# A packed copy of the queries, and a later start, in the recurrent mixer of a two-layer encoder

## The chip, the cores and the metric

One Trainium2 chip; the kernel runs on one of its cores. The metric is the device time of one execution in microseconds (us). Engines are named as the profile names them: PE is TensorE (matmuls; PEld its weight loads), DVE is VectorE, ACT is ScalarE, POOL is GpSimd, SP is SyncE, whose queue issues the loads of weights.

## The reference, cut to what matters

Two sequences, of 512 and 256 tokens (768 together), run through the same trunk of two layers with a model width of 1024, all in fp32. A layer adds half a SwiGLU feed-forward block, a token mixer and again half a feed-forward block to the residual x. The mixer of layer 0 is a bidirectional gated linear recurrence (HGRN2) with 8 heads of 128; that of layer 1 is windowed attention. Of the recurrence, in one direction and for one head:

```python
q, i, g, f_fw, f_bw = jnp.split(x @ w_in, 5, axis=-1)
f = lbd + (1.0 - lbd) * jax.nn.sigmoid(fpre)      # the gate of one direction
k = 1.0 - f
# S_t = diag(f_t) S_{t-1} + k_t v_t^T,  o_t = S_t^T q_t
o = o_fwd + rev(o_bwd)                            # the same, run from the other end
```

So o_t is a sum over all tokens s: the product of q_t and k_s, weighted by the product of the gates between s and t, times v_s.

## The kernel before, in words

All of the work is one program, unrolled by Python, for 768 tokens in 6 blocks of 128. It is a chain of stages: feed-forward f0, the mixer `hgrn`, f1, f2, windowed attention `swa`, f3. The instructions are written in program order with Python generators that weave pieces of different work; a scheduler then fixes the order on each engine at compile time. It may take a later written instruction first if that one is ready in its model and the earlier one isn't. Waits between engines are set by it as well.

Products of the feed-forward blocks and projections split each fp32 operand in a high and a low part and make three matmuls (`mm3`, lines 260 to 262, high times high, high times low, low times high). Weights come in by DMA (line 151), ACT casts the high part (line 166) and DVE subtracts (line 167); `done` frees a weight and stages the next.

The mixer works head by head. `hgrn_proj` makes for one head the projections for the queries (weights with c0 = 0) and the two gates (c0 = 3 and 4), each for the 512 tokens and then for the 256 tokens. It is a generator: it yields after each two of the eight inner tiles for the 512 tokens (4 pieces, the last one behind the evacuation, line 673) and twice for the 256 tokens (2 pieces). So a head's projection has 3 x 6 = 18 pieces. At its end it makes the gates f, the keys k = 1 - f (line 680) and the products q = qs * f of the queries and the gates (line 681), for two directions, which lie one behind the other in one tile of 2 x 768 columns per partition.

`hgrn_scan` computes the outputs of one head in seven levels. At level l the tokens are taken in groups of J = 2^l: the two halves of each pair of groups see each other through gates multiplied up to there. For that, at each level:

- ACT copies the keys that are wanted, alternating between the two directions in runs of J columns, to `kop` (line 717, in the same tile as the matrix A);
- PE makes the scores of the six blocks of 128 tokens: stationary `kop`, moving `rhs(b)`, which reads the queries directly from q with the same alternating pattern, runs of J columns (line 692, in `scan_scores`). Each of these fp32 matmuls stands as two records in the trace;
- DVE puts the scores into A (line 706 copies at level 0, line 711 copies under a mask);
- at level 0 alone PE also makes the diagonal scores from `kd` and `qs`, which lie in order (line 692 too, put by line 711);
- DVE multiplies q (line 734), k (line 738) and the running products of gates `totals` (line 740) for the next level.

After the levels the keys are transposed (line 754, evacuated by line 755), the states of the blocks are made (line 762, then lines 770 and 773), and the outputs are summed from A, q and the states (line 786). ACT squares them (line 790) and copies them over the values (line 792), DVE reduces the squares (line 793).

`hgrn` weaves: the projection of head 0 is made first, then 4 pieces of the projection of head 1 (`lead`), and then each scan is run with 18 pieces of the feed spread evenly over its eight steps (`weave`); the scan of head 3 has 24 more, as the second half of the values' projection is there. The last scan has the projection of the output gates (`proj_tok("g0", ...)`) beside it.

Tiles named "big" share 21 slots of 6 KB per partition; a tile takes a slot when it is first written and gives it back after its last use. Among them are the 8 tiles of h (the mixer's input), the masks, qk, f, q and k of each head, ka (with kop and A), totals, kT and S.

Of the kernel before, what the change touches and what calls it, by code (L numbers as in the profile page):

```python
# [16 lines left out]
P = 128  # L17
# [5 lines left out]
T = TA + TB  # L23
NBLK = T // P
EPS = 1e-6
HEADS = 8
# [13 lines left out]
RAWBUFS = 4  # L40
SLOTS = 21
RING = 1024
UP = ("p1", "p7", "p2", "p5", "p4", "p6", "p3")
DOWN = ("p1", "p2", "p5", "p4", "p7", "p6", "p3")
FACTOR = {"p1": "b00", "p2": "b10", "p3": "b11", "p4": "t4", "p5": "t1", "p6": "t2", "p7": "t3"}
# [2 lines left out]
class Trunk:  # L48
# [344 lines left out]
    def plan_ffn(self, tag, w1, w2):  # L393
        def up(i):
# [4 lines left out]
            else:  # L399
                self.plan_quad((tag, i), (gate, up), (NC, P), UP)  # L400

# [292 lines left out]
    def hgrn_scan(self, hd, v):  # L694
        nc = self.nc
        h, qs, kd, f, q, k = (hd[n] for n in ("h", "qs", "kd", "f", "q", "k"))
        ka = self.big([P, 2, T])
        kop, A = ka[:, 0, :], ka[:, 1, :]
        totals = self.big([P, 2, T])
        blk = lambda t, b: t[:, b * P : (b + 1) * P]  # L700

        def put(level, pss):
            for s, (off, n) in enumerate(SEQS):
                dst = A[:, off : off + n]
                if level == 0:
                    nc.vector.tensor_copy(dst, pss[s])
                    continue
                nb = n // P
                m = self.masks[:, level, :].unsqueeze(1).to_broadcast([P, nb, P])
                r = lambda t: t.rearrange("p (b j) -> p b j", b=nb)  # L710
                nc.vector.copy_predicated(r(dst), m, r(pss[s]))

        tot, base = f, 0
        for l in range(LEVELS):
            c, J = T >> l, 1 << l
            kv = bass.AP(k.tensor, k.offset, [list(k.ap[0]), [2 * J, c // 2], [T + J, 2], [1, J]])
            nc.scalar.copy(kop.rearrange("p (b g j) -> p b g j", g=2, j=J), kv)

            def rhs(b):
                return bass.AP(  # L720
                    q.tensor, q.offset + b * P, [list(q.ap[0]), [2 * J, P // (2 * J)], [T + J, 2], [1, J]]
                )

            pss = [self.ps(n) for _, n in SEQS]
            self.scan_scores(pss, lambda b: blk(kop, b), rhs)
            put(l, pss)
            if l == 0:
                pss = [self.ps(n) for _, n in SEQS]
                self.scan_scores(pss, lambda b: blk(kd, b), lambda b: blk(qs, b))
                put(LEVELS, pss)  # L730
            part = [list(q.ap[0])]
            both = bass.AP(q.tensor, q.offset, part + [[T + J, 2], [2 * J, c // 2], [1, J]])
            t = bass.AP(tot.tensor, tot.offset + base + 1, [list(tot.ap[0]), [T - 1, 2], [2, c // 2], [0, J]])
            nc.vector.tensor_mul(both, both, t)
            for d in range(2):
                xv = self.halves(k, l, d, d)
                t = tot[:, 1 - d, base + 1 - d : base + c : 2].unsqueeze(2).to_broadcast([P, c // 2, J])
                nc.vector.tensor_mul(xv, xv, t)
            nbase = 0 if l == 0 else base + c
            nc.vector.tensor_mul(  # L740
                totals[:, :, nbase : nbase + c // 2], tot[:, :, base : base + c : 2], tot[:, :, base + 1 : base + c : 2]
            )
            tot, base = totals, nbase
            yield

        F, Bk = 1, 0
        order = ((0, 0), (0, 1), (0, 2), (0, 4), (1, 1), (1, 2), (1, 3), (1, 5))
        kT = self.big([P, 8, P])
        S = self.big([P, 8, P])
        for half in range(2):  # L750
            pt = self.ps()
            for i in range(4):
                d, b = order[half * 4 + i]
                nc.tensor.transpose(pt[:, i * P : (i + 1) * P], blk(k[:, d, :], b), self.ident)
            nc.scalar.copy(kT[:, half * 4 : half * 4 + 4, :], pt.rearrange("p (a b) -> p a b", a=4))
        vb = lambda b: v[b][:, h * P : (h + 1) * P]
        pds = []
        for half in range(2):
            pd = self.ps()
            for i in range(4):  # L760
                d, b = order[half * 4 + i]
                nc.tensor.matmul(pd[:, i * P : (i + 1) * P], kT[:, half * 4 + i, :], vb(b), start=True, stop=True)  # L762
            pds.append(pd)
        state = {}
        for d, steps in ((0, ((0, None), (1, 0), (2, 1), (4, None))), (1, ((3, None), (2, 3), (1, 2), (5, None)))):
            for b, prev in steps:
                i = order.index((d, b))
                ds = pds[d][:, (i % 4) * P : (i % 4 + 1) * P]
                if prev is None:
                    nc.scalar.copy(S[:, i, :], ds)  # L770
                else:
                    dec = totals[:, 1 - d, base + b : base + b + 1]
                    nc.vector.scalar_tensor_tensor(S[:, i, :], S[:, order.index((d, prev)), :], dec, ds, ALU.mult, ALU.add)
                state[(d, b)] = S[:, i, :]
        yield
        pos = [self.ps(n) for _, n in SEQS]
        for b in range(NBLK):
            s, i = (0, b) if b < 4 else (1, b - 4)
            o = pos[s][:, i * P : (i + 1) * P]
            terms = [(blk(A, b), vb(b))]  # L780
            if (0, b - 1) in state and b != 4:
                terms.append((blk(q[:, F, :], b), state[(0, b - 1)]))
            if (1, b + 1) in state and b != 3:
                terms.append((blk(q[:, Bk, :], b), state[(1, b + 1)]))
            for j, (l_, r_) in enumerate(terms):
                nc.tensor.matmul(o, l_, r_, start=(j == 0), stop=(j == len(terms) - 1))  # L786
        for s, (off, n) in enumerate(SEQS):
            nb = n // P
            sq = self.tmp(n)
            nc.scalar.square(sq, pos[s])  # L790
            for b in range(nb):
                nc.scalar.copy(vb(off // P + b), pos[s][:, b * P : (b + 1) * P])
            nc.vector.tensor_reduce(
                self.hss[:, h, off // P : off // P + nb], sq.rearrange("p (b j) -> p b j", b=nb), AX.X, ALU.add
            )
# [25 lines left out]
    def hgrn(self, lb_row, gn_row, next_row):  # L821
        nc = self.nc
# [17 lines left out]
        scan = lambda hd: self.hgrn_scan(hd, vs)  # L840
        heads = [{} for _ in range(HEADS)]

        def stream():
            for h in range(1, HEADS):
                yield from self.hgrn_proj(h, heads[h])
                if h == 4:
                    yield from self.proj_tok("v1", put_v(1))

        feed = stream()
        self.drain(self.hgrn_proj(0, heads[0]))  # L850
        lead = 4
        for _ in range(lead):
            next(feed)
        for h in range(HEADS - 1):
            self.weave(scan(heads[h]), feed, 18 + 24 * (h == 3) - (lead if h == HEADS - 2 else 0))
        self.drain(feed)
        rs = self.cp.tile([P, HEADS, NBLK], F32, name="hrs")

# [446 lines left out]
```

## Time and profile before

| | us |
|---|---|
| median of 3 runs | 2811.67 |
| lowest and highest run | 2811.47, 2812.39 |
| span of the profiled execution (first to last instruction) | 2810.8 |
| PE busy in it | 2781.0 |
| DVE busy | 2171.4 |
| ACT busy | 1321.2 |
| POOL busy | 372.5 |

The time outside the span is taken as 2811.67 - 2810.8 = 0.9 us. Matmuls are pipelined: a record's duration overlaps the next one's, so the rate is read from start to start, and a busy PE isn't necessarily at its peak. In the list of groups and in the timeline, `x12` is a count of records, the text in brackets is the idle time of the engine before the first of them and what ended it. The mixer's scans lie between about 572 and 953 us.

### The profile page before, as it was taken

How to read it: one execution, taken by the hardware profiler on the slowest of the kernel's cores; microseconds unless marked ns; L12 is line 12 of the kernel's file. 1: busy time of each engine (PE TensorE's matmuls, PEld its weight loads, DVE VectorE, ACT ScalarE, POOL GpSimd, SP SyncE). 2: the span in 40 equal slices, each digit the busy share in tenths (PEclk: the TensorE clock that was granted, in tenths of full speed). 3: DMA queues.
4: the chain of work that ended last, by engine and by line, in shares of the span. 5: the costliest groups of instructions: out<-in, count | busy, mean ns of one | idle time of the engine just before them, and what ended most of it. 6: DMA issues, size and time to landing. Idle time of an engine off the chain costs nothing.

```text
span 2810.8 us, 40561 instructions
## 1 busy us (share of the span) xinstructions
PE 2781.0 (99%) x15225; PEld 2557.5 (91%) x15225; DVE 2171.4 (77%) x3760; ACT 1321.2 (47%) x2447; POOL 372.5 (13%) x402
## 2 busy tenths in 40 slices
PE   8999999999999999999999999999999899999998
PEld 8999999889899889999999999999888789999998
DVE  8788788477577558878878887887848878878877
ACT  7444444434344336444444644444457756444443
POOL 2111120000000001111111111111102211211110
PEclk9999999999999999999999999999999999999999
DMA  6554464311111133555454355545422013555543
GB/s 174 127 128 120 113 147 123 106 44 38 46 38 38 61 98 76 136 132 126 117 129 120 76 142 132 124 116 124 135 72 76 33 50 83 143 134 125 119 114 108
DMA packets 330100, 291.37 MB, mean 104 GB/s; under 512 B 11608, under 2 KB 257840, under 8 KB 329904
## 3 DMA queue, kind: packets, MB, share of 16 engines
q1 hardware_dynamic: 293920, 212.37, 26.0%
q0 software_dynamic: 31680, 62.93, 13.0%
q10 hardware_dynamic: 4304, 13.49, 1.4%
q8 instruction: 119, 1.95, 0.3%
q14 instruction: 77, 0.63, 0.1%
HBM read 216.39 MB, written 9.44 MB: 80 GB/s over the span
## 4 chain that ended last, share of the span: by engine, by line
PE 95%; ACT 2%; DVE 2%; POOL 0%; issue 0%; DMA 0%; ACTq 0%; DVEq 0%; POOLq 0%
PE ps L436 41%; PE ps L500 20%; PE ps L262 8%; PE ps L260 8%; PE ps L261 8%; PE ps L692 3%; PE ps L786 1%; PE ps L330 1%; PE ps L762 1%; ACT big L1145 1%; PE ps L1167 1%; POOL big L1161 0%; PE ps L1129 0%; PE ps L931 0%; DVE x L522 0%
## 5 line engine op out<-in xcount | busy, mean ns | idle before, releaser
L436 PE MATMUL ps<-big,w 128*128 128x384 f32 x6720 | 1169.3, 334 | 0.0
L436 PEld LDWEIGHTS ps<-big,w 128*128 128x128 f32 x6720 | 1165.9, 188 | 1.7 <-ACT tA L453 0.2
L199 ACT CAST w<-wr 128x512 fp32r<-128x512 f32 x600 | 416.2, 707 | 687.2 <-PE ps L436 277.8
L500 PE MATMUL ps<-w,big 128*128 128x512 f32 x2520 | 575.3, 389 | 0.0
L500 PEld LDWEIGHTS ps<-w,big 128*128 128x128 f32 x2520 | 472.7, 188 | 97.5
L200 DVE TENSOR_TENSOR w<-wr,w 128x512 fp32r<-128x512 f32 (+1 forms) x520 | 434.7, 840 | 146.6 <-ACT w L199 130.8
L522 DVE SCALAR_TENSOR_TENSOR x<-ps,x 128x512 f32<-128x512 f32 x468 | 301.8, 682 | 10.0 <-PE ps L262 9.9
L141 POOL DMA_DIRECT2D s<-wr x120 | 105.9, 882 | 1511.1 <-DMA wr<-in_ffn_w_dram 643.0
L260 PE MATMUL ps<-w,big 128*128 128x512 f32 x624 | 249.3, 400 | 0.3
L262 PE MATMUL ps<-w,big 128*128 128x512 f32 x624 | 244.8, 392 | 2.1 <-DVE big L1005 1.1
L261 PE MATMUL ps<-w,big 128*128 128x512 f32 x624 | 244.0, 391 | 0.0
L260 PE MATMUL ps<-big,w 128*128 128x384 f32 (+2 forms) x640 | 220.4, 346 | 0.5 <-ACT w L166 0.4
L261 PE MATMUL ps<-big,w 128*128 128x384 f32 (+2 forms) x640 | 216.2, 338 | 0.2
L262 PE MATMUL ps<-big,w 128*128 128x384 f32 (+2 forms) x640 | 215.3, 336 | 0.0
L265 ACT CAST big<-tA 128x384 fp32r<-128x384 f32 x296 | 148.0, 513 | 114.0 <-DVE tA L475 36.2
L167 DVE TENSOR_TENSOR w<-wr,w 128x1024 fp32r<-128x1024 f32 x92 | 111.8, 1221 | 83.9 <-ACT w L166 78.5
L266 DVE TENSOR_TENSOR big<-tA,big 128x384 fp32r<-128x384 f32 x296 | 164.7, 567 | 6.7 <-ACT big L265 4.5
L200 POOL TENSOR_TENSOR w<-wr,w 128x512 fp32r<-128x512 f32 x80 | 135.4, 1692 | 202.6 <-ACT w L199 202.6
L166 ACT CAST w<-wr 128x1024 fp32r<-128x1024 f32 x92 | 96.6, 1052 | 122.2 <-PE ps L261 100.6
L206 DVE TENSOR_TENSOR wr<-wr,wr 128x512 f32<-128x512 f32 (+1 forms) x120 | 127.1, 1059 | 21.8 <-issue 20.8
L262 PEld LDWEIGHTS ps<-w,big 128*128 128x128 f32 x624 | 117.1, 188 | 28.5 <-DVE big L1005 1.9
L141 POOL DMA_DIRECT2D wr<-wr x100 | 88.1, 881 | 405.0 <-DVE w L200 166.5
(174 smaller groups left out, 3279.1 us busy)
## 6 DMA issues: line engine op xcount, KB each, us to landing
wr<-in_ffn_w_dram SPq DMA_DIRECT2D x264, 512.0 KB, 4.0
s<-in_ffn_w_dram SPq DMA_DIRECT2D x120, 256.0 KB, 3.2
s<-wr POOLq DMA_DIRECT2D x120, 256.0 KB, 4.9
wr<-wr POOLq DMA_DIRECT2D x80, 256.0 KB, 3.8
wr<-in_hg_w_in_dram SPq DMA_DIRECT2D x40, 512.0 KB, 3.8
wr<-wr POOLq DMA_DIRECT2D x20, 512.0 KB, 4.6
spill<-x ACTq DMA_DIRECT2D x12, 512.0 KB, 3.1
x<-spill ACTq DMA_DIRECT2D x12, 512.0 KB, 3.3
```

Of the source, the lines that this page charges most:

```text
L141: self.nc.gpsimd.dma_start(out, src, accum_op=ALU.add)
L199: nc.scalar.copy(h, src)
L200: (eng or nc.vector).tensor_sub(l, src, h.bitcast(F32))
L206: add = {"second": lambda: nc.vector.tensor_add(a11, a11, a21), "fourth": lambda: nc.vector.tensor_add(a12, a12, a11)}
L260: nc.tensor.matmul(out, a[0], b[0], start=first, stop=False)
L261: nc.tensor.matmul(out, a[0], b[1], start=False, stop=False)
L262: nc.tensor.matmul(out, a[1], b[0], start=False, stop=last)
L265: self.nc.scalar.copy(hi, src)
L266: self.nc.vector.tensor_sub(lo, src, hi.bitcast(F32))
L436: self.nc.tensor.matmul(ps, a[x], b[y], start=first and k == 0 and i == 0, stop=k == 3 and i == 2, skip_group_check=True,)
L500: nc.tensor.matmul(ps, a[x], w[y], start=name == chain and kp == 0 and q == 0, stop=kp == 1 and q == 2, skip_group_check=True,)
L522: self.nc.vector.scalar_tensor_tensor(x, ps, c, x, ALU.mult, ALU.add)
```

## The change

At the levels with J <= PACKED = 1, ACT makes a second copy: the queries, picked by the same pattern as the keys, into a new tile `qop`. The scores of that level then take their moving operand from `qop`, in order, instead of from q. At the other levels nothing changes.

Ahead of the first scan 6 pieces of the feed are run instead of 4, and the first scan weaves 16 pieces instead of 18, so that behind it the feed stands where it stood. With 6 pieces, the projection of head 1 for c0 = 0 is complete, its second evacuation included, and its weights are freed, before the first scan begins.

```diff
+PACKED = 1
...
+        def picked(t, J):
+            return bass.AP(t.tensor, t.offset, [list(t.ap[0]), [2 * J, T // (2 * J)], [T + J, 2], [1, J]])
+
+        def packed(t, J):
+            return t.rearrange("p (b g j) -> p b g j", g=2, j=J)
+
         tot, base = f, 0
         for l in range(LEVELS):
             c, J = T >> l, 1 << l
-            kv = bass.AP(k.tensor, k.offset, [list(k.ap[0]), [2 * J, c // 2], [T + J, 2], [1, J]])
-            nc.scalar.copy(kop.rearrange("p (b g j) -> p b g j", g=2, j=J), kv)
+            nc.scalar.copy(packed(kop, J), picked(k, J))
+            if J <= PACKED:
+                qop = self.big([P, T])
+                nc.scalar.copy(packed(qop, J), picked(q, J))
 
             def rhs(b):
+                if J <= PACKED:
+                    return blk(qop, b)
                 return bass.AP(
                     q.tensor, q.offset + b * P, [list(q.ap[0]), [2 * J, P // (2 * J)], [T + J, 2], [1, J]]
                 )
...
-        lead = 4
-        for _ in range(lead):
+        lead, early = 4, 2
+        for _ in range(lead + early):
             next(feed)
         for h in range(HEADS - 1):
-            self.weave(scan(heads[h]), feed, 18 + 24 * (h == 3) - (lead if h == HEADS - 2 else 0))
+            pieces = 18 + 24 * (h == 3) - (lead if h == HEADS - 2 else 0) - (early if h == 0 else 0)
+            self.weave(scan(heads[h]), feed, pieces)
         self.drain(feed)
```

## The prediction, made before the change was run

> **What bounds the kernel now.** I read the page first: its header, the busy times and the chain that ended last. The profiled execution has a span of 2810.8 us against a median of 2811.67 us of the runs, so 0.9 us lie around the span; every sum below is made in the span, and its difference is taken from the median.
>
> ```profile
> span 2810.8 us, 40561 instructions
> PE 2781.0 (99%) x15225; PEld 2557.5 (91%) x15225; DVE 2171.4 (77%) x3760; ACT 1321.2 (47%) x2447; POOL 372.5 (13%) x402
> PE 95%; ACT 2%; DVE 2%; POOL 0%; issue 0%; DMA 0%; ACTq 0%; DVEq 0%; POOLq 0%
> ```
>
> TensorE (PE) is busy 99% and carries 95% of the chain. A change pays here only by taking time from PE's own instructions or from the few places where PE waits, and it costs only where it makes PE wait. Next I read the chain in order of time, around the mixer's first two scans (line 692 holds the score matmuls; two matmul records make one fp32 matmul, so 12 records are the six blocks of one level).
>
> ```profile
> 571.91 0.24 PE ps L262
> 572.17 0.60 ACT big L673
> 572.77 1.06 ACT big L717
> 573.88 4.81 PE ps L692 x24
> ...
> 614.88 3.12 PE ps L786 x28
> 618.00 3.33 PE ps L692 x24
> ...
> 625.60 1.44 PE ps L692 x12
> 629.78 1.34 PE ps L692 x12
> 633.93 1.34 PE ps L692 x12
> ```
>
> The reader is to see two things. First, level 0 (x24: 12 records on the interleaved queries, 12 for the diagonal) costs 3.33 us at head 1, level 1 1.44, later levels 1.34. Second, at head 0 the chain leaves PE for ScalarE (ACT) before level 0, and that level then takes 4.81. The timeline of PE splits the 3.33, and shows the wait:
>
> ```profile
> 571.75 0.39 PE L262 MATMUL ps<-big,w 128*128 128x512 f32 x1
> 573.88 0.42 PE L692 MATMUL ps<-big,big 128*128 128x128 f32 x1 [1.74 <-ACT big L717]
> 578.45 0.36 PE L260 MATMUL ps<-big,w 128*128 128x256 f32 x1
> 617.84 2.16 PE L692 MATMUL ps<-big,big 128*128 128x128 f32 x12
> 619.83 1.51 PE L692 MATMUL ps<-big 128*128 128x128 f32 x12
> 621.09 0.36 PE L260 MATMUL ps<-big,w 128*128 128x256 f32 x1
> ```
>
> From start to start, 12 records on interleaved queries take 619.83 - 617.84 = 1.99 us, 0.166 each. The diagonal's, whose operands both lie in order, are the rest of the 3.33: 1.34.
>
> **The queries, packed.** The guard is J <= 1, and J is 1 only at l = 0, so just the first pass of the loop is packed (the second scores per head if the diagonal is counted first), in all eight heads. Its moving operand now lies as the diagonal's does, so I give it the diagonal's price: 1.99 - 1.34 = 0.65 us less per head. In seven heads whose level 0 runs at full clock that is 7 x 0.65 = 4.6 us; head 0 is summed apart. The bounds are 0 (were the 0.166 not due to the moving operand) and 0.65.
>
> What it adds is one ACT copy per head of the pattern that line 717 reads. Whether that reaches PE is read from ACT's timeline at a change of heads:
>
> ```profile
> 614.91 0.60 ACT L673 ACTIVATE big<-ps 128x512 f32<-128x512 f32 x1 [0.73 <-PE ps L262]
> 615.41 1.17 ACT L717 COPY big<-big 128x768 f32<-128x768 f32 x1
> 617.14 0.60 ACT L790 ACTIVATE tA<-ps 128x512 f32<-128x512 f32 x1 [0.57 <-PE ps L786]
> 617.64 0.77 ACT L792 COPY x<-ps 128x128 f32<-128x128 f32 x4
> 618.26 0.44 ACT L790 ACTIVATE tB<-ps 128x256 f32<-128x256 f32 x1
> 618.53 0.49 ACT L792 COPY x<-ps 128x128 f32<-128x128 f32 x2
> 620.08 0.93 ACT L717 COPY big<-big 128x768 f32<-128x768 f32 x1 [1.05 <-issue]
> ```
>
> The key copy takes 1.17 us at J = 1 (0.93 at J = 2). Each ACT row starts about 0.1 before the previous one ends, so the query copy would run from 616.5 to 617.65, and PE wants it at 617.84: no wait, with 0.2 us to spare. Half of it fills the 0.57 us in which ACT sat idle; the other half pushes the previous head's squares and copies (lines 790, 792) by about 0.5 us. Behind those wait the reductions on VectorE (DVE) and the next key copy, which had 1.05 us idle before it and is not used until 625.60. So that push ends in slack. The line 734 multiply, which overwrites q, has now to wait for the copy and no longer for 12 matmuls. Later levels keep their margin, for example:
>
> ```profile
> 627.56 0.94 DVE L734 TENSOR_TENSOR big<-big,big 128x768 f32<-128x768 f32 x1
> 631.20 0.84 ACT L717 COPY big<-big 128x768 f32<-128x768 f32 x1 [3.24 <-PE ps L692]
> ```
>
> The key copy ends at 632.04 for scores at 633.93, the multiply at 628.50 for scores at 629.78: 1.9 and 1.3 us. Their chain starts at the scores before, so it moves with PE and doesn't run out when PE is faster.
>
> The copy needs a slot of the 21 "big" ones. At this moment I count 8 for h, 1 for the masks, 4 for this head, kop and totals, the next head's qk, and the previous head's A, q and S: 17. The previous kT and totals were read for the last time by line 762 and by line 773:
>
> ```profile
> 611.93 0.89 PE ps L762 x8
> 613.16 0.73 DVE L773 SCALAR_TENSOR_TENSOR big<-big,big,ps 128x128 f32<-128x128 f32 x2 [0.53 <-ACT big L770]
> ```
>
> Both ended before 614, so a slot is free, and the next head's f, q and k come only when level 0 has given it back.
>
> **The later start of the first scan.** Before, PE issues its last projection matmul at 571.75 and the first score at 573.88, because ACT evacuates the fourth piece (line 673) and only then copies the keys. Two more pieces now stand between: the 256-column half of the same weights, 24 matmuls. In the old order they ran behind level 0; at head 1 the same 24 take from 621.09 to 624.05, 2.96 us; in mid-stream they are 0.12 apart, 2.88.
>
> ```profile
> 621.41 0.28 PE L262 MATMUL ps<-big,w 128*128 128x256 f32 x1
> 621.53 0.28 PE L260 MATMUL ps<-big,w 128*128 128x256 f32 x1
> ...
> 624.05 0.40 PE L260 MATMUL ps<-big,w 128*128 128x512 f32 x1
> ```
>
> PE is then occupied to 571.75 + 2.88 = 574.63. On ACT the key copy ends at 573.83 (572.77 + 1.06 in the chain) and the query copy, another 1.17 less the 0.1 of overlap, at 574.9. PE waits about 0.3 us where it waited 2.13. The second price of that wait is the clock, read from the windows:
>
> ```profile
> 572.00:574.00 2.00, 0.26 (x2) 0.13 (x2) 0.37 (x2) 1.65 (x2) 0.00 (x0) 1.00 0.04 12
> 574.00:576.00 2.00, 2.00 (x11) 2.00 (x12) 1.23 (x3) 0.00 (x0) 0.00 (x0) 0.69 0.00 0
> 576.00:579.00 3.00, 3.00 (x19) 3.00 (x18) 2.37 (x5) 0.92 (x1) 0.00 (x0) 0.64 0.00 0
> ```
>
> Right behind the wait the granted clock is 0.69 and 0.64, and level 0 takes 578.45 - 573.88 = 4.57 us instead of head 1's 3.25 from start to start (617.84 to 621.09): 1.3 us. With 0.3 us of waiting I expect no such drop; head 0 saves 1.83 (wait) + 1.3 (clock) + 0.65 (packing) = 3.8, at most 4.1 without any wait, 2.5 if the clock drops all the same.
>
> [...]
>
> The later start takes two pieces out of head 0's weave: 2 for each of the eight steps, 16, where the rule gave 3, 2, 2, 2, 3, 2, 2, 2. Two pieces cover a level already (the 629.78 and 633.93 rows above), so I cost this at nothing; were a step not covered, it would lose at most the missing piece, 1.4 us. The weights' release, cast and next DMA come 7 us sooner for one key; DMA has 0% of the chain.
>
> **Sum.** 4.6 + 3.8 = 8.4 us: 2811.7 - 8.4 = 2803.3 us.
>
> **The rivals.** (1) The first scan's copies stand behind the new pieces' own evacuation and weight cast on ACT, which come earlier in the program. The last of the 24 matmuls ends at 574.9; with an evacuation below the 0.60 us of the wider one ACT would get to the keys at about 575.3 and end both copies, 1.17 and 1.07 us, at 577.5: PE waits 2.9 us instead of 2.13, with the slow clock again. Head 0 then gives 0.65 - 0.8, about nothing, and the total is 4.6 - 0.2: 2807.3. For it: line 673 stands ahead of line 717 in the old order, and ACT sat idle before it. Against: 24 matmuls now lie between the two evacuations, room for both copies, and at head 1 the key copy is taken as soon as line 673 is done.
>
> (2) The query copy is placed behind the previous head's squares and copies, again earlier in the program. It would start at 618.9 and end at 620.1, and PE, wanting it at 617.84, would wait 2.3 us in each of six changes of heads: 13.8 lost against 4.6 + 3.8 won, 2817; with a clock drop of 1.3 behind each, up to 2825. It turns into a loss from 1.4 us of waiting per head (8.4 / 6). Against it: in the rows above line 717 of the next head already passes lines 790 and 792, and ACT has nothing ready for 0.57 us behind it.
>
> (3) The copy buys nothing, as the 0.166 us comes from something else of level 0. Then only head 0's 3.1 us of wait and clock remain: 2808.6. Against it: level 1, interleaved in pairs, costs 1.44, levels interleaved in fours and more 1.34, a series that fits the reading of the moving operand.
>
> (4) The spare 0.2 us is not there, and every head waits 0.2 to 0.5 us at level 0: 1.4 to 3.5 of the gain go, 2804.7 to 2806.8.
>
> **How the numbers follow.** The forecast has 0.58, rival 1 0.13, rival 2 0.14, rival 3 0.05, rival 4 0.10. The range runs from 2801.5 (no wait at head 0, and 1.5 us for a schedule that falls out better) to 2809.0, which takes in rivals 1, 3 and 4 and leaves out rival 2 and some of the low side. A measurement of this kernel tells about 0.2% from no change, 5.6 us. Faster than 2806.1 are the forecast and most of rival 4: 0.64. Within 0.2% are rivals 1 and 3, and the rest of 4: 0.22. Slower: rival 2, 0.14.
>
> **What would show it.** In the profile after: line 692 at level 0 near 2.7 us for 24 records in every head; a second ACT copy of about 1.17 us right behind the first line 717 row of each head and ahead of line 790; PE idle on ACT before the first score near 0.3 us instead of 1.74; a granted clock of 1.00 behind it. A wait of PE on the query copy of over 1 us at changes of heads, or a slow clock there, would make the forecast wrong; level-0 records still 0.166 apart would make its first term wrong.

## The result, and the profile after

The changed kernel takes 2807.64 us (median of 18 runs, 2805.79 to 2808.97). The kernel before, run beside it each time, takes 2812.49 us (18 runs, 2811.17 to 2814.49; the three runs that the prediction started from lie in the lower part of these). The ratio is 0.9981, 95% interval 0.9974 to 0.9987: 4.85 us less, 0.17%. The interval leaves out 1, but the difference is inside the 0.2% that the prediction called no change. The forecast was 8.4 us less, so 3.5 us are missing.

The page of the changed kernel, the rows that answer to the first ones of before:

```profile
span 2806.4 us, 40557 instructions
PE 2775.5 (99%) x15225; PEld 2551.2 (91%) x15225; DVE 2161.0 (77%) x3760; ACT 1329.5 (47%) x2455; POOL 372.7 (13%) x402
PE 95%; ACT 2%; DVE 2%; DMA 0%; POOL 0%; issue 0%; DVEq 0%; ACTq 0%; POOLq 0%
```

TensorE (PE) still carries 95% of the chain, with 5.5 us less busy time; ScalarE (ACT) has the eight copies more (2455 instructions for 2447) and 8.3 us more. The lines of the code have moved: the scores are line 693 now, the key copy 723, the query copy 726, the evacuation 674.

The chain of the changed kernel (start, duration, what), at the same places as before and at one that is new:

```profile
575.72 2.94 PE ps L693 x24
...
598.19 0.36 issue
598.55 0.83 ACT big L723
599.43 1.60 PE ps L693 x12
...
616.82 2.68 PE ps L693 x24
...
944.45 3.12 PE ps L797 x28
```

Three readings. Level 0 of head 1 takes 2.68 us where it took 3.33. The first scan's level 0 no longer has ACT ahead of it, and takes 2.94 where it took 4.81. But between levels 4 and 5 of that first scan the chain now leaves PE, for a key copy: that was not there before. From level 0 of head 1 to the last output matmuls of the last scan it is 944.45 - 616.82 = 327.63 us; before, the same stretch ran from 618.00 to 950.28:

```profile
950.28 3.12 PE ps L786 x28
```

which is 332.28, so heads 1 to 7 give 4.65 us.

The timeline of PE in the changed kernel (start, duration; in brackets the idle time ahead and what ended it):

```profile
575.44 0.28 PE L263 MATMUL ps<-big,w 128*128 128x256 f32 x1
575.71 1.60 PE L693 MATMUL ps<-big,big 128*128 128x128 f32 x12
...
578.41 0.48 PE L261 MATMUL ps<-big,w 128*128 128x512 f32 x1
...
597.63 0.39 PE L263 MATMUL ps<-big,w 128*128 128x512 f32 x1
599.43 1.60 PE L693 MATMUL ps<-big,big 128*128 128x128 f32 x12 [1.41 <-ACT big L723]
600.79 0.36 PE L261 MATMUL ps<-big,w 128*128 128x256 f32 x1
...
616.65 1.50 PE L693 MATMUL ps<-big,big 128*128 128x128 f32 x12
617.99 1.50 PE L693 MATMUL ps<-big 128*128 128x128 f32 x12
619.25 0.36 PE L261 MATMUL ps<-big,w 128*128 128x256 f32 x1
```

The first score starts 0.27 us after the last projection matmul, and these start 0.12 apart: 0.15 us are lost, where it was 2.13 us from start to start. Level 0 then runs from 575.71 to 578.41, 2.70 us for 4.57; at head 1 it is 619.25 - 616.65 = 2.60. At the new wait, the matmul before starts at 597.63, and its kind are 0.23 apart: the scores start 1.57 us late, 0.16 more than the idle time in brackets, since the last matmul's end is no idle time. The level then takes 600.79 - 599.43 = 1.36 us where the 12 of the diagonal (617.99 to 619.25) take 1.26. In all 1.67 us. The granted clock (the column behind POOL's) in the same windows says why it is no slower than at head 1:

```profile
574.00:576.00 2.00, 2.00 (x17) 1.81 (x16) 0.31 (x1) 2.00 (x3) 0.00 (x0) 1.00 0.00 0
576.00:579.00 3.00, 3.00 (x27) 2.91 (x27) 3.00 (x5) 1.94 (x3) 0.00 (x0) 1.00 0.02 5
598.00:600.00 2.00, 0.59 (x6) 0.58 (x6) 0.85 (x4) 1.32 (x2) 0.00 (x0) 1.00 0.00 0
```

1.00 where it was 0.69 and 0.64; and 1.00 also around the new wait. ACT's timeline of the changed kernel shows the order of the copies:

```profile
573.38 1.18 ACT L723 COPY big<-big 128x768 f32<-128x768 f32 x1
574.47 1.19 ACT L726 COPY big<-big 128x768 f32<-128x768 f32 x1
575.64 1.05 ACT L167 CAST w<-wr 128x1024 fp32r<-128x1024 f32 x1
...
614.22 1.17 ACT L723 COPY big<-big 128x768 f32<-128x768 f32 x1
615.29 1.18 ACT L726 COPY big<-big 128x768 f32<-128x768 f32 x1
616.36 0.60 ACT L801 ACTIVATE tA<-ps 128x512 f32<-128x512 f32 x1
```

At both places the query copy follows the key copy, ahead of the new pieces' cast and of the previous head's squares. At head 1 it ends at 615.29 + 1.18 = 616.47, and PE's scores start at 616.65: 0.18 us to spare.

**Where the time came from and went.** I measure all scans in one stretch: from the start of PE's 2000th matmul record, in the feed-forward block f0 ahead of the mixer, to that of its 5600th, behind the last one. It takes 599.84 us before and 593.32 after: 6.52 less. The stretch from there to the 15200th record takes 1813.69 before and 1815.13 after, 1.44 more, though nothing in it was changed; the rest of the program adds 0.7. Both numbers are followed below.

### The profile page after: what moved, and what is told of

It reads as the page before. It is cut to its first block, busy times and chain, and to the rows that moved or that the text cites. A ratio compares the mean times of both kernels' runs of the same rounds, so it can differ in the third digit from the quotient of the medians.

```text
span 2806.4 us, 40557 instructions
## 1 busy us (share of the span) xinstructions
PE 2775.5 (99%) x15225; PEld 2551.2 (91%) x15225; DVE 2161.0 (77%) x3760; ACT 1329.5 (47%) x2455; POOL 372.7 (13%) x402
## 4 chain that ended last, share of the span: by engine, by line
PE 95%; ACT 2%; DVE 2%; DMA 0%; POOL 0%; issue 0%; DVEq 0%; ACTq 0%; POOLq 0%
PE ps L437 42%; PE ps L501 20%; PE ps L263 8%; PE ps L261 8%; PE ps L262 8%; PE ps L693 3%; PE ps L797 1%; PE ps L773 1%; PE ps L331 1%; PE ps L1179 1%; ACT big L1157 0%; PE ps L1141 0%; POOL big L1173 0%; PE ps L943 0%; PE ps L1192 0%
## 5 line engine op out<-in xcount | busy, mean ns | idle before, releaser
L501 PEld LDWEIGHTS ps<-w,big 128*128 128x128 f32 x2520 | 472.7, 188 | 97.5
L263 PEld LDWEIGHTS ps<-w,big 128*128 128x128 f32 x624 | 117.4, 188 | 28.5 <-DVE big L1017 2.0
L261 PEld LDWEIGHTS ps<-w,big 128*128 128x128 f32 x624 | 117.8, 189 | 22.3 <-ACT w L167 0.3
```

The lines of the kernel that those rows point to most:

```text
L261: nc.tensor.matmul(out, a[0], b[0], start=first, stop=False)
L263: nc.tensor.matmul(out, a[1], b[0], start=False, stop=last)
L501: nc.tensor.matmul(ps, a[x], w[y], start=name == chain and kp == 0 and q == 0, stop=kp == 1 and q == 2, skip_group_check=True,)
```

## The experiments

Theory A: packing gives 0.65 us per head, the later start takes away the first scan's wait and its slow clock, and it costs the new wait between levels 4 and 5 of head 0, because the step lost its third piece while VectorE (DVE) has other work there. Theory B put the new wait down to the query copies, which push ACT's and DVE's work. A third possibility was rival 4, that the query copy itself still costs time at changes of heads.

**1. The packing alone.** The first scan starts where it did.

```diff
-        lead, early = 4, 2
+        lead, early = 4, 0
```

> The queries of level 0 packed, the first scan started after 4 pieces as before. Theory A (the missing 1.9 us come from the step between levels 4 and 5 of head 0, where the later start leaves 2 pieces instead of 3): no PE wait there; seven heads give 0.65 us each, head 0 waits 1.07 us longer for the second copy and gets it back in part: 4.0 to 4.6 us faster than before, with the slow clock behind the first wait. Theory B (the query copy on ScalarE delays the key copies, and so makes that wait): the wait of about 1.4 us stands in this kernel too, and only about 3 us are won.

Measured: 2808.56 us (11 runs; before beside it 2813.35), ratio 0.9986 (0.9977 to 0.9995). Its scans take 3.81 us less than before's, a little under the 4.0 to 4.6 expected. Its chain at the first scan:

```profile
572.62 1.05 ACT big L723
573.68 1.08 ACT big L726
574.80 4.57 PE ps L693 x24
```

Both copies lie on the chain, PE waits 2.8 us, and the window from 574 to 579 us has a granted clock of 0.66. There is no wait between levels 4 and 5: the query copies alone don't make it. Theory B falls here.

**2. The later start alone.**

```diff
-PACKED = 1
+PACKED = 0
```

> Only the later start, queries read interleaved at all levels. Theory A: the first wait (1.9 us) and the slow clock behind it (1.3) go, a PE wait of about 1.4 us with 0.3 of restart comes between levels 4 and 5 of head 0: 1.5 us faster than before. Theory B: no such wait, 3.2 us faster.

Measured: 2813.11 us (11 runs), ratio 1.0000 (0.9991 to 1.0009); scans 1.39 us less, near the 1.5 of theory A. The runs don't show that gain: in the profile the stretch behind the scans takes 1.5 us more than before's, of a kind that experiment 9 follows. The first scan's wait is gone, and the waits of PE on this line are one:

```profile
PE ps L693 <- ACT big L723: 1.4, 1, 1.4
```

(in all, times, longest). The new wait belongs to the later start, as A has it. Alone, it takes back 1.67 of the 3.1 us that the start gives.

**3. The third piece back** (called the third kernel below). The weave counts the two early pieces as used, so that its eight steps take 1, 2, 2, 2, 3, 2, 2, 2 pieces where the change has 2 in each.

```diff
-    def weave(main, feed, pieces, steps=LEVELS + 1):
-        used = 0
+    def weave(main, feed, pieces, steps=LEVELS + 1, used=0):
...
-            pieces = 18 + 24 * (h == 3) - (lead if h == HEADS - 2 else 0) - (early if h == 0 else 0)
-            self.weave(scan(heads[h]), feed, pieces)
+            pieces = 18 + 24 * (h == 3) - (lead if h == HEADS - 2 else 0)
+            self.weave(scan(heads[h]), feed, pieces, used=early if h == 0 else 0)
```

> The whole change, but the 16 pieces of the first scan are spread 1, 2, 2, 2, 3, 2, 2, 2 (the old 18 without the first two) instead of 2 in each step. Theory A: no PE wait between levels 4 and 5 of head 0, 1.7 us less than the changed kernel, some 6.5 us faster than before; level 1 has one piece less in front of it, and its operands were 1.1 us early enough. Theory B: the wait stays near 1.4 us and the time is that of the changed kernel.

Measured: 2806.38 us (9 runs), ratio 0.9976 (0.9967 to 0.9986). In the scans PE waits nowhere; they take 7.76 us less than before's, 1.24 better than the change's 6.52. What the weave does beside covering is seen in DVE's timeline, here of the changed kernel, then of this one (whose lines are one lower):

```profile
591.36 1.20 DVE L168 TENSOR_TENSOR w<-wr,w 128x1024 fp32r<-128x1024 f32 x1
...
592.81 0.95 DVE L745 TENSOR_TENSOR big<-big,big 128x768 f32<-128x768 f32 x1
593.68 0.67 DVE L680 TENSOR_SCALAR big<-big,lb_buf 128x768 f32<-128x768 f32 x1
...
594.44 0.95 DVE L682 TENSOR_TENSOR big<-big,big 128x768 f32<-128x768 f32 x1
595.30 1.06 DVE L712 COPY_PREDICATED big<-big,ps 128x512 f32<-128x512 uint8 x2
596.25 0.95 DVE L745 TENSOR_TENSOR big<-big,big 128x768 f32<-128x768 f32 x1
597.12 1.02 DVE L749 TENSOR_TENSOR big<-big,big 128x384 f32<-128x384 f32 x2
```

```profile
591.50 1.03 DVE L748 TENSOR_TENSOR big<-big,big 128x384 f32<-128x384 f32 x2
592.45 1.22 DVE L168 TENSOR_TENSOR w<-wr,w 128x1024 fp32r<-128x1024 f32 x1
...
595.40 0.68 DVE L679 TENSOR_SCALAR big<-big,lb_buf 128x768 f32<-128x768 f32 x1
```

Line 749 (here 748) multiplies the keys, which the next level's key copy waits for. With the pieces spread as before, it stands ahead of the weight subtraction (168) and of the next head's gates (680 and 682, here 679 and 681). In the change, counted with the two early ones, 4, 6, 8 and 10 pieces have run after the first four steps instead of 3, 5, 7 and 9; the subtraction and the gates go with the pieces, come earlier, and stand ahead of that multiply. DVE then works without a gap from 590.7 to 598.25, the multiply ends at 598.14, and the key copy starts at 598.55, when PE has run out of its two pieces.

**4. VectorE relieved instead.** One weight subtraction of the step goes to GpSimd (POOL); the pieces stay as in the change.

```diff
-            self.nc.vector.tensor_sub(lo, raw, hi.bitcast(F32))
+            (self.nc.gpsimd if key == ("hgrn", 2, 4) else self.nc.vector).tensor_sub(lo, raw, hi.bitcast(F32))
```

> The whole change with its 2 pieces per step, but one weight's subtraction (1.2 us on VectorE, the one that falls between levels 3 and 4 of head 0) is made on GpSimd. If VectorE's backlog makes the wait between levels 4 and 5, the key multiply comes 1.2 us earlier and the PE wait falls from 1.4 us to under 0.5. If the evacuation in front of the key copy on ScalarE makes it, the wait stays between 1.0 and 1.4 us.

Measured: 2807.30 us (11 runs), ratio 0.9979 (0.9970 to 0.9988); scans 7.18 us less than before's. The wait of 1.4 is gone, though the step still has 2 pieces, and one of 0.4 us appears one level earlier. DVE and POOL in this kernel:

```profile
590.94 2.41 DVE L745 TENSOR_TENSOR big<-big,big 128x768 f32<-128x768 f32 x1
...
594.90 1.01 DVE L749 TENSOR_TENSOR big<-big,big 128x384 f32<-128x384 f32 x2
```

```profile
590.13 2.40 POOL L168 TENSOR_TENSOR w<-wr,w 128x1024 fp32r<-128x1024 f32 x1 [79.30 <-ACT w L167]
```

The keys' multiply ends at 595.91, and the copy is ready in time. So DVE's backlog is shown as a cause, beside the spread of the pieces: mend either, and the wait goes. Part of the gain is lost to something new: the multiply of line 745, beside POOL's subtraction, takes 2.41 us for 0.95, and PE waits 0.4 us for it.

**5. No query copy.** Level 0's scores read the first half of q, in order; this leaves out the other direction's queries at that level, and the copy.

```diff
-            if J <= PACKED:
-                qop = self.big([P, T])
-                nc.scalar.copy(packed(qop, J), picked(q, J))
...
-                    return blk(qop, b)
+                    return blk(q[:, 0, :], b)
```

> The changed kernel without the query copy: level 0 reads the queries of one direction in order, straight from q, so the other direction's queries are left out of level 0. Theory A (the copy costs nothing beside 0.15 us at the first scan): the time of the changed kernel within 0.5 us. If the copy costs 0.2 to 0.5 us in each head: 1.4 to 3.5 us faster than the changed kernel.

Measured: 2807.86 us (10 runs), ratio 0.9980 (0.9971 to 0.9989); scans 6.54 us less than before's, against the change's 6.52. The copy costs nothing: rival 4 falls.

**6. The copy twice.**

```diff
                 nc.scalar.copy(packed(qop, J), picked(q, J))
+                nc.scalar.copy(packed(qop, J), picked(q, J))
```

> The changed kernel with the query copy made twice, one behind the other. In its trace the copy ends 0.35 us before PE wants it at a change of heads, and the second ends 1.08 later. Theory A (the copy is hidden by a margin of 0.35 us): PE waits 0.7 us at each change of heads and 1.2 at the first scan, 5 to 6 us slower than the changed kernel. Rival (there is more room, as work of PE can be put in front): under 1 us slower. Rival (it is on the path already): 1.08 us in eight heads, 8.6 us slower.

Measured: 2816.45 us (10 runs), ratio 1.0011 (1.0002 to 1.0020); scans 8.9 us longer than the change's. ACT, then PE, at head 1:

```profile
616.86 1.17 ACT L727 COPY big<-big 128x768 f32<-128x768 f32 x1
```

```profile
618.07 1.60 PE L693 MATMUL ps<-big,big 128*128 128x128 f32 x12 [0.91 <-ACT big L727]
```

PE sits idle at the first scan for 1.22 us and in each of six further heads for 0.91, 6.7 us in all, and each wait costs 0.26 us beyond its idle time, as the new one of the change does (in the chain the level takes 2.94 for 2.68), 1.8 in all: 8.5 of the 8.9. My expectation of 5 to 6 us was smaller since it took the chain's start of the level, 616.82, for that of the scores, 616.65 (the spare time is 0.18 us, not 0.35), and since it left out the 0.26. The total lies near the 8.6 us of the last rival there, a copy that is on the path already; but 0.91 is about what the 1.08 of a second copy leaves after 0.18 to spare, and experiment 5, which takes the copy away and gains nothing, rules that rival out. So one copy of 1.17 us just fits, and a second doesn't.

**7. Two levels packed,** on the third kernel.

```diff
-PACKED = 1
+PACKED = 2
```

> The kernel with the pieces spread 1, 2, 2, 2, 3, 2, 2, 2, and the queries packed at level 1 (J = 2) too. If the moving operand's runs set the matmul's rate: level 1 goes from 1.44 to 1.34 us in each head, 0.8 us in all, and the extra ScalarE copy (0.93 us) ends some 1.5 us before PE wants it. If packing pays at runs of one column alone: no gain at level 1, and the same time within 0.3 us in the traced scans.

Measured: 2806.97 us (10 runs), ratio 0.9975 (0.9966 to 0.9985); scans 0.9 us longer than the third kernel's. Level 1 falls from 1.44 to 1.34 us where nothing is in the way. At head 3, which weaves 42 pieces, something is (ACT's timeline; here line 673 is the evacuation and 725 the query copy):

```profile
710.11 0.60 ACT L673 ACTIVATE big<-ps 128x512 f32<-128x512 f32 x1 [4.25 <-PE ps L263]
710.61 0.90 ACT L725 COPY big<-big 128x768 f32<-128x768 f32 x1
```

The copy stands in ACT's queue behind an evacuation that waits for the last of the pieces, and PE waits 1.48 us for it: more than the seven tenths that the other heads give. This is the failure that rivals 1 and 2 described for level 0, found at another level.

**8. Two levels packed but at head 3,** on the same kernel; the condition changes at both places where it stands.

```diff
-            if J <= PACKED:
+            if J <= PACKED - (h == 3):
```

> The same spread, queries packed at levels 0 and 1, but at level 0 alone in head 3, where the copy of level 1 stood behind an evacuation and made PE wait 1.5 us. If that wait was all that the second copy cost: 0.1 us less in seven heads and no wait, 0.7 us faster than the spread alone in the traced scans, 8.4 less than before. If the copies delay something else as well: no faster than the spread alone.

Measured: 2805.26 us (10 runs), ratio 0.9975 (0.9965 to 0.9984); scans 8.50 us less than before's, the least of all; one wait of 0.2 us is left in them. In the runs it can't be told from the third kernel.

**9. The three kernels again:** before in a single run, and the change and the third kernel side by side on one chip.

> The kernel before, unchanged, for one more profile. If the slow clock behind the first scan's wait of 1.7 us comes in every execution, level 0 of head 0 takes 4.6 us again; if it depends on when the wait falls, as the same wait of 2.3 us in the attention stage was followed by a slow clock in three of six profiles, it may take 3.3 here and the slow clock may stand behind another wait.

> The changed kernel, unchanged, beside the two below on one chip: 5 to 6.5 us faster than before, PE wait of 1.4 us between levels 4 and 5 of head 0.

> The kernel with the pieces spread 1, 2, 2, 2, 3, 2, 2, 2 again: by the traced scans (7.8 us less than before against 6.5) 1.2 us faster than the changed kernel, 6.5 to 7.8 faster than before.

Measured: before 2815.02 us in its one run. PE waits 1.74 us at its first scan again, and level 0 takes 4.76 in the chain, so the slow clock came again too. After 2807.87 us (11 runs; before beside it 2812.76), ratio 0.9982 (0.9973 to 0.9991), 4.9 us less, just under the 5 to 6.5 expected; the third kernel 2805.43 (9 runs), ratio 0.9976 (0.9966 to 0.9986), 2.4 us under the change, though the intervals overlap. Scans against the first profile of before: after 6.03 less, the third kernel 8.03 less, before again 0.26 more. The scans thus repeat within half a microsecond, and this half lies ahead of them, where the mixer begins: from PE's 2700th record on, amid the projections (516.80 us before), the change gives 6.55 and 6.49 us, the third kernel 8.08 and 8.07, and before again differs by 0.10. What doesn't repeat is the rest, up to the 15200th record: 1815.54 for before, 1816.53 for after, 1813.63 for the third kernel. The windows show where. The attention stage has two places where PE sits idle for longer, one behind two waits with a short matmul between them, one behind a single wait (PE's timeline in the changed kernel):

```profile
2197.66 0.33 PE L1179 MATMUL ps<-ident_r,big 128*128 128x128 f32 x1 [1.27 <-POOL big L1173]
2198.90 0.33 PE L1179 MATMUL ps<-ident_r,big 128*128 128x128 f32 x1 [0.68 <-POOL big L1173]
...
2242.43 0.53 PE L943 MATMUL ps<-ident_r,big 128*128 128x128 f32 x4 [1.87 <-DVE big L267]
```

The windows around them, of the changed kernel and then of the third kernel run again (the granted clock is the number behind POOL's count):

```profile
2195.00:2215.00 20.00, 15.05 (x82) 10.92 (x81) 18.08 (x51) 15.88 (x42) 5.90 (x9) 1.00 0.30 105
2240.00:2262.00 22.00, 19.86 (x110) 16.52 (x109) 18.00 (x50) 15.85 (x42) 6.73 (x12) 0.92 0.17 49
```

```profile
2195.00:2215.00 20.00, 15.92 (x86) 12.00 (x86) 18.03 (x54) 14.89 (x41) 5.35 (x10) 1.00 0.24 79
2240.00:2262.00 22.00, 21.47 (x128) 18.36 (x129) 18.34 (x56) 16.07 (x46) 6.76 (x12) 1.00 0.16 47
```

In 13 profiles of ten programs the granted clock drops in 4 at the first place and in 4 at the second; with two levels packed it drops once more, 14 us behind the first place. In 7 profiles it drops at none of them. (The three of six in the expectation for before counts both places: behind the 2.3 us from start to start at the second, 2240.16 to 2242.43 in the change, it was two of those six.) By the number of drops the rest takes a median of 1813.7 us (none, 7 profiles), 1815.2 (one, 3) and 1816.3 (two, 3): 1.3 to 1.5 us for each drop.

All these drops, and those at the first scan, are alike: the granted clock is 0.50 for 3.41 us (at the first scan before, from 574.77 to 578.18), and then 1.00 again. Each begins a whole number of 3.41 us slots behind the clock's first rise in its profile (at the first scan before, 574.77 - 14.99 = 559.78 us, 164 slots of 3.413; in the change, 2244.45 - 12.14 = 2232.31, 654 of them). The runs scatter with the clock too, as the mean granted clock of each is on record: in the three sets of runs of before beside the experiments, those with a mean of 0.998 have medians of 2814.2, 2815.0 and 2814.2 us, those with 0.999 have 2812.8, 2812.9 and 2812.7. One drop moves this mean by 0.0006 (half of 3.41 us in 2806), so it is a coarse count.

## Why the prediction was right, and where it was wrong

**The packing: right.** 0.65 us per head and 4.6 for seven were forecast; it is 3.33 - 2.68 = 0.65 and 4.65. Rival 3 falls with it. With the queries read in order straight from q (experiment 5) level 0 takes 2.68 as well, so it is the order of reading that pays, and not the new tile. The prediction's count of slots was wrong without effect: the tiles that it lists add up to 19 of the 21, not 17, and the copy still found its slot.

**The query copy hidden at changes of heads: right.** 616.5 to 617.65 with 0.2 us to spare was the forecast; relative to the scores it ends 0.18 ahead of them. The copy taken away gains nothing, the copy doubled costs 8.9 us in the scans. Rivals 2 and 4 fall.

**The first scan's start: right.** A wait of 0.3 us was expected; PE's gap is 0.27 from start to start, 0.15 of it more than usual, and 0.10 go in the level behind it. The slow clock is gone, and level 0 gave 4.57 - 2.70 = 1.87 for the 1.3 + 0.65 forecast. Rival 1 falls: the new pieces' cast starts at 575.64, behind both copies. The slow rows belong to the wait: with it gone they went too (a granted clock of 1.00 from 574 to 579 us), and with the packing alone, where the wait was 2.8 us, they stayed (0.66).

**The step that failed: "Two pieces cover a level already … so I cost this at nothing".** It is the change's one new wait, 1.41 us of idle time and 0.26 around it: 1.67 us. The rows that I cited for it (629.78 and 633.93) are of other levels of another head; they were no measure of the step behind level 4 of head 0, where before had three pieces. Nor did I see that the same rounding sends other work to DVE earlier, ahead of the keys' multiply. The bound that I set beside it, "at most the missing piece, 1.4 us", was nearly right; it missed the 0.26. ACT's queue may add a part, as the key copy also stands behind an evacuation that waits for the pieces' last matmul (ACT's timeline in the changed kernel):

```profile
598.06 0.60 ACT L674 ACTIVATE big<-ps 128x512 f32<-128x512 f32 x1 [2.83 <-PE ps L263]
598.55 0.82 ACT L723 COPY big<-big 128x768 f32<-128x768 f32 x1
```

The keys were ready at 598.14 and ACT had taken the evacuation at 598.06: without it the copy could have started some 0.4 us sooner. That wasn't tried by itself; with DVE relieved (experiment 4) the key copy ran ahead of this evacuation.

**The sum.** The forecast was 8.4 us in the scans. They gave 6.52: 8.4 - 1.67 = 6.7, with 0.2 that I don't assign. With the third piece back they gave 7.76 and 8.03 (8.08 and 8.07 from the 2700th record). So the working was right but for that one term. The total by itself says little: 2807.64 us lies in the range because this reached up to 2809.0, it lies within 0.2% of no change, to which the prediction gave a chance of 0.22 against 0.64 for more, and it is 0.3 us from the 2807.3 of rival 1, of whose mechanism the trace shows nothing.

**The rest, from 6.5 in the scans to 4.85 in the runs, is not settled.** The attention stage of both profiles of the change had a slow clock behind its waits, that of one of two of before, that of neither of the third kernel. One such drop costs 1.3 to 1.5 us, near the size of what is missing, and drops are at least a part of why runs of one kernel spread over 2.4 to 6 us. The waits there are nearly the same in every kernel (1.3, 0.7 and 1.9 us of idle time), and the runs give no sign that the change has more drops: 4 of its 29 have a mean clock of 0.998, against 21 of the 81 of before beside the experiments.

Another part may lie in the prediction's 1.3 us for the first scan's clock. Both profiles of before have that drop, but a wait of 1.74 us fits into one slot of 3.41 us from only about half of the places where it can begin (1.67 of 3.41). That a drop needs the whole wait in one slot is not shown; by this estimate of mine some executions of before would go without the drop, and there the later start would give 1.3 us less. It would fit this that in all ten sets of runs of kernels without that wait the gain is 0.5 to 1.7 us smaller than in their traced scans, and 1.0 us larger with the packing alone, which keeps a wait; no run shows it directly. The prediction took the drop as there in every execution of before, and had no term for drops elsewhere.

## What to carry to other kernels

When work is moved between two places, price the place it leaves: look there at each step in turn for what its neighbours do, not at a like step elsewhere, and count the pieces per step as the rounding gives them, with the work that they send to the other engines, and not by their sum. Where several changes of about 1 us are judged, read the stretch that they touch in the profile; the whole run's time also has the scatter of waits that nothing touched.

## What the runs showed of the hardware

**The clock behind waits.** The 12 drops that the 13 profiles have ahead of the program's end are all of the same form, 0.50 for 3.41 us from the edge of a slot. Where the slots lie changes from one execution to the next: the clock first rises 14.99 us into the program in one profile of before, and 12.10 us in the other (12.14 in the first of the change). In the slot right ahead of a drop PE was busy for 0.18 to 0.51 of the time in 11 of the 12, and for 0.62 in one; four more slots of 0.47 to 0.51 were not followed by one. In the change both kinds stand: 1.75 us busy of 3.41 from 2241.04, with a drop behind it, and 1.75 of 3.41 from 2196.67, with none. So the drops came behind slots with much idle time, but the busy share of a slot doesn't settle whether one comes. At the first scan, idle times of 1.74 us (from 2.1 us between starts) to 2.8 us were followed by the drop in 3 of 3 profiles, at a cost of some 1.3 us. The wait of 1.4 us never was, in 5 of 5; with the copy doubled, the one of 1.22 and the six of 0.91 us were not either. In the attention stage, the pair of 1.27 and 0.68 us was followed by it in 4 of 13 profiles, and the wait of 1.87 us in 4 of 13.

**The moving operand.** Score records took 0.166 us each, from start to start, with runs of one column (1.99 us for the 12 of level 0 before), 0.120 with runs of two (1.44 us for level 1), and 0.112 in order and with runs of four and more (1.34 us). Runs of two are thus 7% slower than the latter, and packing them took that away (experiment 7).

**What a wait costs beyond its idle time.** 0.26 us on PE at the new wait of the change, at a granted clock of 1.00: 0.16 because the records before it overlap (0.39 us long, 0.23 apart), and 0.10 in the level behind it.

**A DVE multiply beside a POOL subtraction.** In experiment 4 a DVE multiply with two inputs took 2.41 us for 0.95 while POOL subtracted beside it: the two overlapped from 590.94 to 592.53, 1.59 us, and the multiply lost 1.46. It is one such pair; why the multiply lost that is not shown.
